# Running the first delta-rule chunks beside the input projection's last three column tiles

## The chip, the cores and the metric

One core of a Trainium2 chip runs the whole kernel. The metric is the device time of one execution in microseconds (us). A change counts as faster or slower here when two kernels, run alternately on the same chip, differ by more than what their runs scatter.

## The reference

The kernel computes one layer of a hybrid encoder for 16 + 2048 prompt rows and 64 sample rows, together 2128 rows. Cut to what matters here:

```python
h = rms_norm(x, attn_norm)
z = einsum('bld,dc->blc', h, w_in)          # ONE input projection
q_lat, kv_lat, k_rope_raw, qkv, gate, beta, a = split(z)
q = einsum(rms_norm(q_lat), w_uq)           # 8 attention heads
attn = chunk_causal_attention(q, k, v)      # k, v from kv_lat
u, k, v = causal_conv_silu(qkv) ...         # gated delta rule ("gdn")
for each chunk i:                           # a scan over the rows
    v_new = u_i - w_i @ S
    o     = (q_i * exp(g_i)) @ S + qk_i @ v_new
    S     = S * exp(g_last) + (k_i * exp(g_last - g_i)).T @ v_new
gdn = rms_norm(o) * silu(gate)
x = x + concat[rms_norm(attn), gdn] @ w_out
y = x + square(relu(rms_norm(x) @ w_up)) @ w_down
```

u, w and qk of a chunk come out of a triangular system of the chunk's own keys (its inverse is built by doubling), so they can be prepared ahead of the scan; only S runs from chunk to chunk.

## The kernel before

Matrix products are done in split numbers: each float operand is a high and a low part, and a product is three matmuls (high by high, high by low, low by high).

**The projection** (`phase_a`). The rows lie in five blocks of 336, 512, 512, 512 and 256. The 22 column tiles of the weight (128 columns each) are worked off in batches, in the order of the list `BATCHES`; for each batch a loop runs over the five blocks, and within a block over the batch's column tiles. `col_product` makes one column tile of one block: 8 x 3 = 24 matmuls into one PSUM bank `ps`. `col_finish` evicts it (L282, VectorE: `zt<-ps,rstd`), and for the output gate's tiles 17 to 20 a SiLU follows (three ScalarE activations L369 to L371, one VectorE product L372) and a store to `scr_gateT`. Tiles 0 to 2, the query latent, are followed by a norm: sums of squares, `mean_rstd` (a matmul into the small PSUM tile `ps_n`, L241), `rsqrt` (L141 to L146), three scalings (L325) and three stores to `scr_qlatT`. The six `zt` buffers go round, so an eviction waits until the store that last read its buffer is done. PSUM has eight banks: six go to `ps` (`APB`), two to `ps_n`. The last batches are `[0, 1, 2], [18], [19], [20]`: three times the five blocks, one gate tile after the other. `load_w` loads a column tile's weight in two halves (`wraw`), scales it (L258) and splits it (L134 on ScalarE, L135 on VectorE).

**The delta rule** (`phase_g`). 18 chunks are worked off by Python generators that are stepped round by round: `gdn_prep` (all that a chunk needs ahead of the scan: its keys' transposes L455, decay L461, norms L458 and L469, normed keys `kn` L485 and their transposes L489, products L498, the doubling with the tables `lev` L511 to L557, and at last `uf`), `gdn_scan` (the scan's first matmul is L598), and `q_gen`, the attention's queries (17 tiles x 18 matmuls L728 to L730 from the weight `wuq` and the stored query latent). Matmul results of `gdn_prep` go to five PSUM banks `gpp`, of the scan to two `gps`, and of `q_gen` to one `qp`. `q_gen`'s matmuls do not depend on the chunks and fill gaps. Attention, the output projection and the MLP follow.

**Who sets the order.** The Tile framework builds one instruction queue for each engine. A scheduler at build time sorts by dependencies and priorities (the order in which the program was written, if nothing else is said). On the chip each engine runs its queue in order: an instruction that waits holds up all behind it. Tiles come from pools. A pool that closes gives its SBUF or PSUM to pools opened later, whose first tiles then wait for the last reader of the old ones. In the kernel before, phase A's pools all close at its end, so `gpp` and most of the delta rule's SBUF take the place of the projection's.

Of the kernel before, what the change touches and what calls it, by code (L numbers as in the profile page):

```python
# [8 lines left out]
F32 = mybir.dt.float32  # L9
# [32 lines left out]
BATCHES = [[21, 3, 4]] + [[5 + i] for i in range(12)] + [[17], [0, 1, 2], [18], [19], [20]]  # L42
# [5 lines left out]
      "kneg": 3, "bh": 4, "bl": 4, "tt": 5, "uu": 5, "q16": 2, "rk": 3, "se": 1, "vw": 2, "S": 3, "o1": 1, "o": 1, "fr": 2}  # L48
GR, GK, GA, GF, GL0 = 6, 4, 5, 2, 4
QSB, QS = 2, 5  # L50
# [68 lines left out]
class Prog:  # L119
# [42 lines left out]
    def phase_a(self):  # L162
        nc, I = self.nc, self.I
        with ExitStack() as es:
# [7 lines left out]
            self.hp = self.pool(es, "h")  # L172
# [3 lines left out]
            self.aps = self.pool(es, "aps", space=PSUM)  # L176
# [35 lines left out]
    def load_x(self, b):  # L212
# [4 lines left out]
        hi = self.hp.tile([128, 8, n], F32R, name=f"hhi{b}")  # L217
        lo = self.hp.tile([128, 8, n], F32R, name=f"hlo{b}")
# [43 lines left out]
    def col_product(self, w, b):  # L262
# [5 lines left out]
        ps = self.aps.tile([128, NB], F32, name="ps", tag="ps", bufs=APB)  # L268
# [163 lines left out]
    def gt(self, tag, bufs=1, shape=(128, 4, 128), dt=F32):  # L432
        return self.gp.tile(list(shape), dt, name=tag, tag=tag, bufs=GB.get(tag, 1))

    def gpsum(self, kind="p"):
        return self.gps.tile([128, 4, 128], F32, name="gp" + kind, tag="gp" + kind, bufs=GPS[kind])
# [211 lines left out]
    def phase_g(self, g=True, q=True, eb=None):  # L648

        with ExitStack() as es:  # L650
            eq = es.enter_context(ExitStack())
            qp = self.pool(eq, "q", side="right")
            qps = self.pool(eq, "q_ps", space=PSUM, side="right")
            self.gp = self.pool(es, "g")
            self.gps = self.pool(es, "gps", space=PSUM)
            self.state = None
            self.lev = [[self.gp.tile([128, 4, 128], F16, name=f"lev{j}{i}") for i in range(7)] for j in range(NL)]
# [7 lines left out]
            while g and scanned < len(CHUNKS):  # L665

                if rounds >= max((started - GF) * GR, began[started % NL] + GL0) and len(preps) < GK and started < min(len(CHUNKS), scanned + GA):
                    preps.append(self.gdn_prep(CHUNKS[started], Ps[started]))
                    began[started % NL] = rounds
                    started += 1  # L670
                rounds += 1
                if rounds > QS:
                    if ek is not None:
                        if next(ek, "x") == "x" and self.first_prep is None:
                            self.first_prep = self.prep((0, 0, 0))
                            next(self.first_prep)
                    elif next(qg, "x") == "x" and eb is not None:
                        eq.close()
                        self.attn_early(eb)
                        ek = self.early_keys = self.keys(0, 0)  # L680
                if scan is None and "uf" in Ps[scanned]:
                    scan = self.gdn_scan(CHUNKS[scanned], Ps[scanned])
                if scan is not None and next(scan, "x") == "x":
                    scan, scanned = None, scanned + 1
                for p in list(preps):
                    if next(p, "x") == "x":
                        preps.remove(p)
# [346 lines left out]
    def attention(self):  # L1034
        with ExitStack() as es:
# [58 lines left out]
            while prep and prep[0][2] == 0:  # L1094
                prep_step()
# [835 lines left out]
```

## Time and profile before

| | |
|---|---|
| median of 3 runs | 3327.87 us (3316.88 to 3330.03) |
| the profiled execution | 3322.66 us |
| its span, first to last instruction | 3320.9 us |
| TensorE (PE) busy | 96% of the span |
| VectorE (DVE) busy | 80% |
| ScalarE (ACT) busy | 47% |
| GpSimd (POOL) busy | 12% |
| TensorE's granted clock, mean | 0.979 of 2.4 GHz |

TensorE is busy nearly all the time, but "busy" also holds time at half clock, in which the same work takes twice as long. In a row of the trace, the number in brackets at the end is how long the engine stood idle just before, and what released it.

### The profile page before, as it was taken

Reading aid. Unit: us, or ns where it says so; the run is one execution under the profiler, and the core shown is the slowest. Engines: PE = TensorE matmul, PEld = TensorE weight load, DVE = VectorE, ACT = ScalarE, POOL = GpSimd, SP = SyncE. Lnnn points to the kernel's source line nnn. Section 1 sums busy time; section 2 is a strip of 40 time slices with the busy share of each in tenths; the row PEclk is TensorE's granted clock in tenths of the full one; section 3 lists DMA queues with packets and bytes.
Section 4 is the critical chain, followed back from the end, with each engine's and each line's share of the span. In section 5 each row is a group of like instructions: output and inputs, shape, how many; then the busy total and the mean of one; then the engine's idle time right before and its main releaser. Section 6 shows DMA issues by size and latency. Waiting matters only on the chain.

```text
span 3320.9 us, 54512 instructions
## 1 busy us (share of the span) xinstructions
PE 3196.8 (96%) x20037; PEld 2943.1 (89%) x20037; DVE 2650.8 (80%) x5438; ACT 1558.4 (47%) x3495; POOL 400.5 (12%) x758
## 2 busy tenths in 40 slices
PE   9999998998979999999899999999999999999999
PEld 6888887888867778887799999999999999999999
DVE  8877654788758788888789888888888888988887
ACT  5555524555536868787564222334333333422232
POOL 0100013675510000000201000011000002100000
PEclk9999998999978999999999999999999999999999
DMA  4322213233221011010332222233222225122222
GB/s 132 91 74 70 74 63 100 87 104 100 59 57 35 20 34 34 25 37 26 106 99 75 77 77 75 76 110 109 88 76 73 65 73 160 58 73 77 77 74 70
DMA packets 318091, 248.09 MB, mean 75 GB/s; under 512 B 31776, under 2 KB 291616, under 8 KB 317760
## 3 DMA queue, kind: packets, MB, share of 16 engines
q1 hardware_dynamic: 300256, 219.21, 22.8%
q10 hardware_dynamic: 15536, 16.23, 1.6%
q0 software_dynamic: 2032, 9.18, 0.8%
q8 instruction: 157, 2.57, 0.3%
q14 instruction: 110, 0.90, 0.1%
HBM read 196.99 MB, written 47.52 MB: 74 GB/s over the span
## 4 chain that ended last, share of the span: by engine, by line
PE 83%; DVE 8%; ACT 2%; DMA 2%; issue 2%; POOL 1%; SPq 0%; POOLq 0%; DVEq 0%; ACTq 0%
PE psu L1601 23%; PE psd L1601 21%; PE ps L270 5%; PE ps L271 5%; PE ps L272 5%; PE pss L994 2%; PE pso L1011 2%; PE pss L995 2%; PE pss L996 2%; PE pso L1013 2%; PE pso L1012 2%; PE pspre L964 2%; DVE hl L1581 0%; PE psm L889 0%; DMA qh<-mrow 0%
## 5 line engine op out<-in xcount | busy, mean ns | idle before, releaser
L1601 PE MATMUL psu<-hh,uh 128*128 128x352 f32 x1728 | 563.0, 326 | 2.6 <-ACT uh L1497 2.1
L1601 PE MATMUL psu<-hl,uh 128*128 128x352 f32 x1728 | 557.3, 323 | 0.0
L1601 PE MATMUL psu<-hh,ul 128*128 128x352 f32 x1728 | 549.9, 323 | 0.0
L1601 PE MATMUL psd<-al,dh 128*128 128x352 f32 x1536 | 496.0, 323 | 3.5 <-DVE al L1790 3.2
L1601 PE MATMUL psd<-ah,dl 128*128 128x352 f32 x1536 | 494.6, 322 | 0.0
L1601 PE MATMUL psd<-ah,dh 128*128 128x352 f32 x1536 | 473.3, 324 | 11.1 <-DVE y L1709 7.4
L1709 DVE TENSOR_TENSOR y<-y,psd 128x352 f32<-128x352 f32 x768 | 386.6, 515 | 103.5 <-PE psd L1601 101.5
L1601 PEld LDWEIGHTS psu<-hh,uh 128*128 128x128 f32 x1728 | 325.7, 189 | 4.5 <-ACT uh L1497 2.5
L1601 PEld LDWEIGHTS psu<-hl,uh 128*128 128x128 f32 x1728 | 326.1, 189 | 1.2 <-issue 0.5
L1601 PEld LDWEIGHTS psu<-hh,ul 128*128 128x128 f32 x1728 | 323.9, 188 | 0.2 <-DVE ul L1475 0.2
L270 PE MATMUL ps<-hhi,whi 128*128 128x512 f32 (+5 forms) x880 | 313.6, 360 | 9.7 <-ACT hhi L134 7.1
L272 PE MATMUL ps<-hhi,wlo 128*128 128x512 f32 (+5 forms) x880 | 314.0, 358 | 0.0
L271 PE MATMUL ps<-hlo,whi 128*128 128x512 f32 (+5 forms) x880 | 312.5, 356 | 0.3 <-DVE hlo L135 0.2
L1601 PEld LDWEIGHTS psd<-ah,dh 128*128 128x128 f32 x1536 | 284.1, 188 | 16.9 <-DVE y L1709 11.5
L1601 PEld LDWEIGHTS psd<-al,dh 128*128 128x128 f32 x1536 | 289.1, 188 | 5.5 <-DVE al L1790 5.4
L1497 ACT CAST dh<-wr 128x512 fp32r<-128x512 f32 x192 | 119.3, 621 | 367.2 <-PE psd L1601 324.8
L1601 PEld LDWEIGHTS psd<-ah,dl 128*128 128x128 f32 x1536 | 288.8, 188 | 0.0
L1788 ACT CAST ah<-u 128x352 fp32r<-128x352 f32 x192 | 93.4, 487 | 398.6 <-DVE u L1786 280.0
L135 DVE TENSOR_TENSOR Pl<-P,Ph 128x512 fp32r<-128x512 f32 (+4 forms) x352 | 211.2, 611 | 52.2 <-ACT Ph L134 49.7
L998 ACT ACTIVATE P<-pss 128x512 f32<-128x512 f32 (+4 forms) x352 | 185.9, 539 | 87.6 <-PE pss L996 76.9
L965 DVE TENSOR_REDUCE mp<-pspre 128x1 f32<-128x296 f32 (+6 forms) x400 | 189.1, 500 | 31.1 <-PE pspre L964 29.2
L1714 POOL TENSOR_TENSOR y<-y,v 128x352 f32<-128x352 f32 x40 | 40.8, 1043 | 1330.8 <-DVE y L1709 1330.7
(458 smaller groups left out, 7266.5 us busy)
## 6 DMA issues: line engine op xcount, KB each, us to landing
wr<-in_w_up SPq DMA_DIRECT2D x192, 256.0 KB
wr<-in_w_down SPq DMA_DIRECT2D x192, 256.0 KB
qn<-scr_qN SPq DMA_DIRECT2D x32, 384.0 KB
wr<-in_w_out SPq DMA_DIRECT2D x48, 256.0 KB
wraw<-in_w_in SPq DMA_DIRECT2D x42, 256.0 KB
scr_convT<-s SPq DMA_DIRECT2D x36, 256.0 KB
mixr<-scr_mixT SPq DMA_DIRECT2D x12, 704.0 KB
out_y_T<-y SPq DMA_DIRECT2D x48, 176.0 KB
```

The costliest lines, as they stand in the source:

```text
L135: (lo_eng or nc.vector).tensor_tensor(lo, src, hi.bitcast(F32), op=ALU.subtract)
L270: nc.tensor.matmul(ps[:m, :n], whi[:, k, :m], hi[:, k], start=k == 0, stop=False)
L271: nc.tensor.matmul(ps[:m, :n], whi[:, k, :m], lo[:, k], start=False, stop=False)
L272: nc.tensor.matmul(ps[:m, :n], wlo[:, k, :m], hi[:, k], start=False, stop=k == 7)
L964: nc.tensor.matmul(ps[:, :z - a], qh[:r, i * 128:(i + 1) * 128], kh[:r, a:z], start=True, stop=True)
L965: nc.vector.tensor_reduce(m[:, i:i + 1] if one else mp[:, j:j + 1], ps[:, :z - a], axis=AX.X, op=ALU.max)
L994: nc.tensor.matmul(ps[:w, off:], kh[:r, s:s + w], qh[:r, off:], start=True, stop=False)
L998: nc.scalar.activation(p[:w, off:], ps[:w, off:], AF.Exp)
L1497: self.nc.scalar.copy(t[0], src)
L1601: self.nc.tensor.matmul(ps, w, h, start=i == 0, stop=i == len(steps) - 1)
L1709: adds.append(nc.vector.tensor_tensor(Y[j][:, d], Y[j][:, d], ps, op=ALU.add).ins)
L1788: done = nc.scalar.copy(A[f, j][0], u).ins
```

## The change

The three gate tiles 18, 19 and 20 become one batch, so that its loop goes block by block: tiles 18, 19, 20 of block 0, then of block 1, and so on. Their products no longer go into the six `ps` banks: that pool is closed ahead of the batch, and the products share the two banks of `ps_n`, in a pool on the other side of PSUM. So the delta rule's five `gpp` banks can be given out while the batch still runs. The split rows of each block (`hhi`, `hlo`) get a pool of their own, so that the SBUF of blocks 0, 1 and 2 comes free as the batch passes them; some buffers of the delta rule (the table `EG`) lie there, in the pool `g_early`. The scheduler gets a high priority for the first 2 steps of `q_gen` and the first 12 rounds of the delta rule, and another for the attention's first preparation.

```diff
-BATCHES = ... + [[17], [0, 1, 2], [18], [19], [20]]
+BATCHES = ... + [[17], [0, 1, 2], [18, 19, 20]]
+EG = {"kv": 2, "kq": 3, "lg": 1, "ss": 3, "sq": 1, "dm": 2, ...}
+HR, HO = 12, 360
+AO = 150
...
-            self.hp = self.pool(es, "h")
+            self.hp = [self.pool(es, f"h{b}") for b in range(len(BLOCKS))]
...
-            self.aps = self.pool(es, "aps", space=PSUM)
+            self.apn = self.pool(es, "apn", space=PSUM, side="right")
+            ea = es.enter_context(ExitStack())
+            self.aps = self.pool(ea, "aps", space=PSUM)
...
+                if not nxt:
+                    ea.close()
                 Wn = [self.load_w(ct) for ct in nxt[:3 - len(batch)]]
...
-                        ps = self.col_product(w, b)
+                        ps = self.col_product(w, b, n + 1 == len(BATCHES))
...
-        ps = self.aps.tile([128, NB], F32, name="ps_n", tag="psn", bufs=2)
+        ps = self.apn.tile([128, NB], F32, name="ps_n", tag="psn", bufs=2)
...
-        ps = self.aps.tile([128, NB], F32, name="ps", tag="ps", bufs=APB)
+        if last:
+            ps = self.apn.tile([128, NB], F32, name="ps", tag="psn", bufs=2)
+        else:
+            ps = self.aps.tile([128, NB], F32, name="ps", tag="ps", bufs=APB)
...
     def gt(self, tag, bufs=1, shape=(128, 4, 128), dt=F32):
-        return self.gp.tile(list(shape), dt, name=tag, tag=tag, bufs=GB.get(tag, 1))
+        k, n, e = self.gcount.get(tag, 0), GB.get(tag, 1), EG.get(tag, 0)
+        self.gcount[tag] = k + 1
+        early = k % n < e
+        return (self.ge if early else self.gp).tile(list(shape), dt, name=tag, tag=tag, bufs=e if early else n - e)
...
-            self.gps = self.pool(es, "gps", space=PSUM)
+            self.gps = {k: self.pool(es, "gp" + k, space=PSUM) for k in "ps"}
...
-            for _ in range(QP):
-                next(qg, None)
+            with self.tc.high_priority(HO):
+                for _ in range(QP):
+                    next(qg, None)
...
+                with ExitStack() as early:
+                    if rounds < HR:
+                        early.enter_context(self.tc.high_priority(HO))
...
-            while prep and prep[0][2] == 0:
-                prep_step()
+            with self.tc.high_priority(AO):
+                while prep and prep[0][2] == 0:
+                    prep_step()
```

Every engine runs the same instructions in both kernels (TensorE 21013 of them, VectorE 5438); only their order, their buffers and their waits differ. Line numbers after the change are 9 to 21 higher. Three places of the built queues show it.

TensorE, where the last batches begin. `ps_4447` is tile 18 of block 0 in the kernel before, `ps_4480` and `ps_4513` are the same tile of blocks 1 and 2; shown are the first matmul of each product and, of the first product, where the norm's matmul stands:

```order
L272 MATMUL ps_4370<-hhi4_772,wlo_3895 128x256
L270 MATMUL ps_4447<-hhi0_126,whi_4423 128x336 [waits DVE_49,Activation_49]
...
L241 MATMUL ps_n_4397<-sq_4308,ones_64 128x512 [waits Pool_49]
...
L270 MATMUL ps_4480<-hhi1_249,whi_4423 128x512
...
L270 MATMUL ps_4513<-hhi2_403,whi_4423 128x512
```

After the change `ps_4475`, `ps_4508` and `ps_4541` are tiles 18, 19 and 20 of block 0, and `ps_4592` and `ps_4625` tiles 18 and 19 of block 1:

```order
L250 MATMUL ps_n_4412<-sq_4323,ones_64 128x512 [waits DVE_49,Pool_49]
L282 MATMUL ps_4475<-hhi0_141,whi_4438 128x336 [waits DVE_49,Activation_49]
...
L282 MATMUL ps_4508<-hhi0_141,whi_4450 128x336 [waits DVE_49,Activation_49]
...
L282 MATMUL ps_4541<-hhi0_141,whi_4462 128x336 [waits DVE_49,Activation_49]
...
L250 MATMUL ps_n_4574<-sq_4430,ones_64 128x256 [waits DVE_49]
L282 MATMUL ps_4592<-hhi1_264,whi_4438 128x512 [waits DVE_49]
...
L282 MATMUL ps_4625<-hhi1_264,whi_4450 128x512 [waits DVE_49]
```

The third product now waits for VectorE (its bank was the first product's), as does every one behind it; before, the second and third products waited for nothing of VectorE's.

VectorE after the change, at the same place. `zt_4500` and `zt_4533` evict tiles 18 and 19 of block 0; the rows ahead belong to the weight of tile 20 and to the query latent's norm:

```order
L151 TENSOR_TENSOR nr_4417<-nr_4417,nt_4415 128x512 [waits DVE_49]
L140 TENSOR_TENSOR wlo_4463<-wraw_4464,whi_4462 128x512 [waits Activation_49]
L140 TENSOR_TENSOR wlo_4463<-wraw_4469,whi_4462 128x512 [waits Activation_49]
L337 SCALAR_TENSOR_TENSOR zt_4249<-zt_4249,g_qa_93,nr_4417 128x512 [waits DVE_49]
L337 SCALAR_TENSOR_TENSOR zt_4276<-zt_4276,g_qa_93,nr_4417 128x512
L337 SCALAR_TENSOR_TENSOR zt_4303<-zt_4303,g_qa_93,nr_4417 128x512
L319 TENSOR_TENSOR sq_4430<-sq_4430,sq_4435 128x256 [waits Activation_49]
L294 TENSOR_TENSOR zt_4500<-ps_4475,rstd_128 128x336 [waits DMAHW7_49,DVE_49,PE_49]
L294 TENSOR_TENSOR zt_4533<-ps_4508,rstd_128 128x336 [waits DMAHW0_49,DVE_49,PE_49]
```

The first eviction of the batch stands behind the same scalings and waits for the same store as in the kernel before (there it is `zt_4472<-ps_4447`, also the 628th row of VectorE's queue); it did not move.

TensorE, where the projection ends and the delta rule begins. Before, `ps_4939` is the last product, `gpp_5021` the first chunk's transposes, `gpp_5095` the transposes of its normed keys, `qp_5319` the first query product:

```order
L270 MATMUL ps_4939<-hhi4_772,whi_4630 128x256 [waits DVE_49]
...
L455 MATMUL gpp_5021<-ident_59,kv_5014 16x128 [waits DMAHW2_49,DVE_49]
...
L461 MATMUL gpp_5076<-m_le_72,lg_5054 128x128 [waits Pool_49]
...
L489 MATMUL gpp_5095<-ident_59,kn_5063 128x16 [waits DVE_49,Activation_49]
...
L728 MATMUL qp_5319<-wuq_h_5004,ql_h_5262 128x384 [waits Activation_49]
```

After the change the same chunk's steps are `gpp_5047` (L470), `gpp_5102` (L476, of the second chunk) and `gpp_5121` (L504); `ps_4823` and `ps_4856` are tiles 19 and 20 of block 3, `ps_4889`, `ps_4922` and `ps_4955` tiles 18 to 20 of block 4, `gpp_5305` the transposes of the third chunk's normed keys, `qp_5345` the first query product, `gps_5745` the first scan:

```order
L470 MATMUL gpp_5047<-ident_59,kv_5040 16x128 [waits DMAHW5_49]
...
L282 MATMUL ps_4823<-hhi3_604,whi_4450 128x512 [waits DVE_49]
...
L476 MATMUL gpp_5102<-m_le_72,lg_5080 128x128 [waits Pool_49]
...
L282 MATMUL ps_4856<-hhi3_604,whi_4462 128x512 [waits DVE_49]
...
L504 MATMUL gpp_5121<-ident_59,kn_5089 128x16 [waits DVE_49,Activation_49]
...
L282 MATMUL ps_4955<-hhi4_787,whi_4462 128x256
...
L504 MATMUL gpp_5305<-ident_59,kn_5278 128x128 [waits DVE_49,Activation_49]
...
L749 MATMUL qp_5345<-wuq_h_5030,ql_h_5288 128x384 [waits Activation_49]
...
L613 MATMUL gps_5745<-vn_5087,uf_5657 16x128
```

The first two chunks' first steps have moved ahead of five of the fifteen products, which now stand between them. The query products moved back: 63 of their matmuls stand ahead of the first scan before, 9 after. The weight `wuq`, which they need, is loaded by SyncE's queue behind three more chunks' keys than before.

## Rows read from the trace of the kernel before

**Rows 1.** Busy us of each engine by stretch of the span, with granted clock:

```profile
core 0: us, PE busy (x) PEld busy (x) DVE busy (x) ACT busy (x) POOL busy (x), PEclk, DMA share, GB/s
450.00:500.00 50.00, 50.00 (x279) 43.98 (x278) 33.07 (x55) 18.88 (x35) 4.30 (x3) 1.00 0.28 99
500.00:530.00 30.00, 30.00 (x153) 25.95 (x152) 7.82 (x13) 11.36 (x20) 0.28 (x1) 1.00 0.25 72
...
540.00:550.00 10.00, 2.05 (x16) 1.59 (x14) 7.28 (x18) 5.13 (x26) 6.41 (x15) 0.82 0.79 247
550.00:560.00 10.00, 9.19 (x45) 8.12 (x45) 6.94 (x13) 4.04 (x8) 6.62 (x6) 0.50 0.43 112
560.00:570.00 10.00, 7.80 (x50) 6.48 (x49) 6.59 (x12) 6.65 (x23) 9.26 (x15) 0.84 0.28 74
570.00:580.00 10.00, 10.00 (x64) 8.52 (x63) 4.06 (x10) 4.43 (x19) 5.64 (x14) 0.65 0.16 31
...
590.00:600.00 10.00, 9.78 (x95) 8.53 (x96) 6.10 (x16) 4.09 (x15) 3.64 (x9) 0.83 0.20 61
```

**Rows 2.** Timeline of TensorE: start us, us, engine, line, operation:

```profile
538.81 0.60 PE L455 MATMUL gpp<-ident,kv 128*16 128x128 f32 x4
...
550.46 0.57 PE L489 MATMUL gpp<-ident,kn 16*128 16x16 f32 x4 [8.11 <-DVE kn L485]
...
565.41 0.40 PE L529 MATMUL gpp<-id,lev 128*128 128x128 f16 x4 [0.95 <-DVE lev L521]
...
569.60 1.08 PE L489 MATMUL gpp<-ident,kn 128*128 128x128 f32 x4 [1.15 <-DVE kn L485]
...
585.82 0.40 PE L529 MATMUL gpp<-id,lev 128*128 128x128 f16 x4 [1.35 <-DVE lev L521]
...
590.19 0.44 PE L728 MATMUL qp<-wuq_h,ql_h 128*128 128x384 f32 x1 [1.07 <-ACT qsq L732]
...
597.27 0.39 PE L598 MATMUL gps<-vn,uf 16*16 16x128 f32 x2
```

**Rows 3.** Timeline of VectorE behind the projection's end:

```profile
541.61 2.10 DVE L511 COPY lev<-id 128x512 f16<-128x512 f16 x10
...
544.45 2.53 DVE L469 TENSOR_SCALAR rk<-ss 16x4 f32<-16x4 f32 x2
549.64 0.68 DVE L485 TENSOR_TENSOR kn<-gpp,rk 16x512 f32<-16x512 f32 x1 [2.66 <-POOL rk L146]
```

**Rows 4.** Groups of TensorE's instructions between 468.76 and 538.81 us:

```profile
L270 PE MATMUL ps<-hhi,whi 128*128 128x512 f32 x72 | 28.2, 392 | 0.0
...
L270 PE MATMUL ps<-hhi,whi 128*128 128x336 f32 x24 | 8.0, 333 | 0.0
...
L270 PE MATMUL ps<-hhi,whi 128*128 128x256 f32 x24 | 6.8, 282 | 0.0
```

**Rows 5.** Timeline of TensorE, first matmul of tile 18:

```profile
468.76 0.32 PE L270 MATMUL ps<-hhi,whi 128*128 128x336 f32 x1
```

**Rows 6.** Timeline of VectorE at that batch's start:

```profile
472.20 1.28 DVE L135 TENSOR_TENSOR wlo<-wraw,whi 128x512 fp32r<-128x512 f32 x2
...
482.28 2.07 DVE L325 SCALAR_TENSOR_TENSOR zt<-zt,g_qa,nr 128x512 f32<-128x512 f32 x3
485.19 0.51 DVE L282 TENSOR_TENSOR zt<-ps,rstd 128x336 f32<-128x336 f32 x1 [0.84 <-DMA scr_qlatT<-zt]
```

**Rows 7.** Timeline of SyncE's queue, DMA issues:

```profile
472.91 0.93 SPq L256 DMA_DIRECT2D wraw<-in_w_in  x2
483.06 1.65 SPq L327 DMA_DIRECT2D scr_qlatT<-zt  x3
...
541.87 0.82 SPq L700 DMA_DIRECT2D qs<-in_w_uq  x2
```

**Rows 8.** Timeline of ScalarE, weight of tile 20:

```profile
477.73 1.27 ACT L134 CAST whi<-wraw 128x512 fp32r<-128x512 f32 x2 [1.62 <-DVE wraw L258]
```

**Rows 9.** Timeline of ScalarE, query weight's high part:

```profile
552.60 1.57 ACT L134 CAST wuq_h<-qs 128x768 fp32r<-128x768 f32 x2
```

More of the change, by code (lines that the diff above doesn't have):

```diff
@@ L41 @@
 RUNS = [(0, 1), (1, NS), (NS, NS + 1), (NS + 1, 18)]
-BATCHES = [[21, 3, 4]] + [[5 + i] for i in range(12)] + [[17], [0, 1, 2], [18], [19], [20]]
+BATCHES = [[21, 3, 4]] + [[5 + i] for i in range(12)] + [[17], [0, 1, 2], [18, 19, 20]]
 WRB, APB, ZTB, XTB = 2, 6, 6, 4
@@ L216, in load_x @@
         n = b1 - b0
-        hi = self.hp.tile([128, 8, n], F32R, name=f"hhi{b}")
-        lo = self.hp.tile([128, 8, n], F32R, name=f"hlo{b}")
+        hi = self.hp[b].tile([128, 8, n], F32R, name=f"hhi{b}")
+        lo = self.hp[b].tile([128, 8, n], F32R, name=f"hlo{b}")
         self.h.append((hi, lo))
@@ L260, in load_w, with col_product @@
         return hi, lo, m
-    def col_product(self, w, b):
+    def col_product(self, w, b, last=False):
         nc = self.nc
@@ L432, in gt @@
     def gt(self, tag, bufs=1, shape=(128, 4, 128), dt=F32):
[L433 removed]
+        k, n, e = self.gcount.get(tag, 0), GB.get(tag, 1), EG.get(tag, 0)
+        self.gcount[tag] = k + 1
+        early = k % n < e
+        return (self.ge if early else self.gp).tile(list(shape), dt, name=tag, tag=tag, bufs=e if early else n - e)
     def gpsum(self, kind="p"):
[L436 removed]
+        return self.gps[kind].tile([128, 4, 128], F32, name="gp" + kind, tag="gp" + kind, bufs=GPS[kind])
     def gdn_prep(self, n, P):
@@ L653, in phase_g @@
             qps = self.pool(eq, "q_ps", space=PSUM, side="right")
+            self.ge, self.gcount = self.pool(es, "g_early"), {}
             self.gp = self.pool(es, "g")
-            self.gps = self.pool(es, "gps", space=PSUM)
+            self.gps = {k: self.pool(es, "gp" + k, space=PSUM) for k in "ps"}
             self.state = None
-            self.lev = [[self.gp.tile([128, 4, 128], F16, name=f"lev{j}{i}") for i in range(7)] for j in range(NL)]
+            self.lev = [[self.ge.tile([128, 4, 128], F16, name=f"lev{j}{i}") for i in range(7)] for j in range(NL)]
             qg = self.q_gen(qp, qps) if q else iter(())
             ek = None
-            for _ in range(QP):
-                next(qg, None)
+            with self.tc.high_priority(HO):
+                for _ in range(QP):
+                    next(qg, None)
             Ps = [{"first": i < NL} for i in range(len(CHUNKS))]
@@ L665, in phase_g @@
             while g and scanned < len(CHUNKS):
[L667 to L687, printed above, removed]
+                with ExitStack() as early:
+                    if rounds < HR:
+                        early.enter_context(self.tc.high_priority(HO))
+                    if rounds >= max((started - GF) * GR, began[started % NL] + GL0) and len(preps) < GK and started < min(len(CHUNKS), scanned + GA):
+                        preps.append(self.gdn_prep(CHUNKS[started], Ps[started]))
+                        began[started % NL] = rounds
+                        started += 1
+                    rounds += 1
+                    if rounds > QS:
+                        if ek is not None:
+                            if next(ek, "x") == "x" and self.first_prep is None:
+                                self.first_prep = self.prep((0, 0, 0))
+                                next(self.first_prep)
+                        elif next(qg, "x") == "x" and eb is not None:
+                            eq.close()
+                            self.attn_early(eb)
+                            ek = self.early_keys = self.keys(0, 0)
+                    if scan is None and "uf" in Ps[scanned]:
+                        scan = self.gdn_scan(CHUNKS[scanned], Ps[scanned])
+                    if scan is not None and next(scan, "x") == "x":
+                        scan, scanned = None, scanned + 1
+                    for p in list(preps):
+                        if next(p, "x") == "x":
+                            preps.remove(p)
```

2 lines of the change are left out of this document (added).

## The prediction

> **What bounds the kernel now.** TensorE is busy for 96% of the span, so a change of order pays only where TensorE stands idle or runs at its lower clock. I read the busy time by stretches first [rows 1]. Up to 530 us TensorE is busy without a gap at granted clock 1.00. From 540 to 550 it is busy for 2.05 of 10 us, and then the clock is 0.50 (1.2 instead of 2.4 GHz) for a whole stretch, and lower than 1.00 in three of the next four. The timeline of TensorE [rows 2] names the place: the projection's last matmul ends where the first chunk's transposes start, at 538.81, and after a few of them the engine stands for 8.11 us until `kn`, the normed keys, arrives from VectorE; `kn` itself ends a chain of small steps over four engines (squares, `rk` at 544.45, GpSimd's `rsqrt`, `kn` at 549.64, with 14 copies of the table `lev` in front of it, the last ten of them from 541.61) [rows 3]. Four more waits of the same kind follow, 0.95, 1.15, 1.35 and 1.07 us, before the first scan starts at 597.27 [rows 2].
>
> **What the change can win.** Between 538.81 and 597.27 the waste is:
> - idle: 8.11 + 0.95 + 1.15 + 1.35 + 1.07 = 12.6 us [rows 2];
> - half clock: of each stretch's busy time, the share of the clock that was not granted: 9.19 x 0.50 + 7.80 x 0.16 + 10.00 x 0.35 + 9.78 x 0.17 = 4.6 + 1.2 + 3.5 + 1.7 = 11.0 us [rows 1].
>
> Together 23.6 us. Since TensorE runs the same matmuls in both kernels, this is all that the start of the delta rule can give back. That 54 of the query's matmuls move behind the first scan is neither gain nor loss in this account: it makes the first scan earlier, and they are done later.
>
> After the change the chain from the first transposes to `kn` lies beside products: between them the queue holds tile 19 of block 3 whole and 14 of the 24 matmuls of tile 20. The price of a product follows from its columns. The fifteen products from 468.76 to 538.81 [rows 4, 5, 2] have 9 x 512 + 3 x 336 + 3 x 256 = 6384 columns in 70.05 us, 0.011 us a column: 5.6 us for 512 columns, 3.7 for 336, 2.8 for 256. So 5.6 x 38/24 = 8.9 us of products and some 2 us of other steps stand where 8.11 us of idle time stood, and I count that wait as gone, with the half clock behind it. `lev`'s copies have moved ahead of the chain.
>
> It is not all gone. From the last product (`ps_4955`) to the first scan the queue now has 9 query matmuls where before they filled the gaps, and the doubling of the first chunks is a chain through VectorE and ScalarE. Waits like the 4.5 us that stood there in spite of the filler [rows 2] will be there again: at least 0, at most twice as much and a stretch at half clock of 3.5 us [rows 1], so 0 to 12; I take 5, near what stood there. That leaves a gain of 18.6 us.
>
> **What the change adds.** The products of the last batch now have two PSUM banks. Follow the start of the batch. Tile 18 of block 0 starts at 468.76 [rows 5] and takes 3.7 us. Tile 19 of block 0 needs the low part of its weight, which VectorE makes from 472.20 to 473.48 [rows 6], and so ends at about 473.4 + 3.7 = 477.1. Tile 20 needs the bank of tile 18, thus its eviction. In the kernel before that eviction comes at 485.19 only [rows 6], 12.7 us after the product's end, and this costs nothing because five more banks are free: TensorE is busy all the time [rows 1]. What it waits for is a store: its `zt` buffer is read by the query latent's store, issued at 483.06 [rows 7] behind the scalings at 482.28 [rows 6], which stand behind a weight of the batch that was issued at 472.91 [rows 7]. In the changed queue of VectorE the same instructions stand in front of it and it waits for the same store, so I see no reason for it to be earlier. Tile 20 starts at 485.19 + 0.51 = 485.7: a new wait of 8.6 us. Behind it the next product, tile 18 of block 1, needs tile 20's eviction, which stands behind two sums of the gate: about 1 us more. From then on a product (5.6 us) is longer than an eviction, and two banks do. Sum: 9.6 us. Of this 1.5 us would be there with any number of banks, as the weight of tile 20 is cast from 477.73 [rows 8].
>
> Bounds: below, only that 1.5 us, if the order on the chip lets the eviction be earlier; above, 12, if each of the next products in block 0 and 1 waits for 1 us too. After the wait I expect a stretch at half clock, as after the 8.11 us: 4.6 us [rows 1], between 0 and the 9.3 that all of 550 to 580 cost. The sum of what is added is 9.6 + 4.6 = 14.2 us.
>
> A rule speaks against the change here. The Trainium skill (Perfetto Trace Analysis, Matmuls and Matmul Optimizations) says that independent groups of matmuls should rotate through the PSUM banks, so that the eviction of one overlaps the next, and that all eight should be used. By that rule alone the sum would be a loss of the 14.2 us. The trace agrees for block 0, where the eviction comes 12.7 us after its product; in later blocks, where it follows within a product's time, no row shows that more than two are needed.
>
> The edits that cost nothing: the pool of each block and `g_early` issue no instructions, and the g phase's buffers lie in blocks that the batch has passed; the priority `AO` leaves the attention's first matmuls where they were; the gate's SiLU and stores are the same in number and lie beside products of 2.8 to 5.6 us (uncovered, an eviction costs what the row of 0.51 us shows, once a product [rows 6]).
>
> **Sum.** 14.2 added - 18.6 won = -4.4 us. Against the profiled execution of 3322.66 us that is 3318.3; the runs' median is 5.2 us higher, and against it 3323.5 us, which is my forecast.
>
> **The rivals.**
> 1. *The wait for the bank is short, or the clock stays up.* For it: the 8.6 us rest on one eviction in a queue of before. Against: the same 627 instructions stand in front. With 1.5 us of wait and no half clock the gain is 18.6 - 1.5 = 17.1; with the idle time but full clock it is 9.0. Faster: 3308 to 3319.
> 2. *Slower: the query's weight comes late and stops VectorE.* In the queue of VectorE the low part of `wuq` stands in the middle of the doubling, and its loads are now issued behind three more chunks' keys. Before, the loads were issued at 541.87 [rows 7] and first used at 552.60 [rows 9], so they may take up to 10.7 us. If the keys' buffer that the last of these loads waits for comes free only when the third chunk is under way, VectorE stands up to 10.7 us with the doubling behind it, and TensorE, which has no filler there, with it, and a half clock stretch of 4.6 follows. That is 15.3 - 4.4 = 11 us slower, 3339; from a standstill of about 3 us on the gain is gone. Two such loads in sequence would pass 0.5%.
> 3. *It does not do what it says*: the first chunks' steps wait for SBUF or keys that come no earlier, and the products merely stand somewhere else: the 8.11 us stay, in several pieces. Then there is the 14.2 us of loss against some of the gain: within 10 us of before, 3330 to 3337.
>
> **How the numbers follow.** Forecast (3317 to 3330) 0.52, rival 1 0.28, rival 2 0.10, rival 3 0.10. About 0.5%, 16.6 us, is what a measurement of this kernel can tell from no change: under 3311.3 is faster, over 3344.5 slower. Rival 1 gives three quarters of its chance to faster, the forecast a little: 0.23. Slower takes half of rival 2 and some of rival 3: 0.08. The rest is the same: 0.69. The range goes from rival 1's better end to where rival 3 ends: 3307 to 3336; outside are the worst of rival 2 and a gain of the whole 23.6 us with scatter.
>
> **What would show it.** In the profile after: a wait of 8 to 9 us of TensorE near 477 us, ended by an eviction of VectorE, with about 1 us behind it and a stretch at half clock from 486 on; the first transposes of the delta rule near 533 instead of 538.81, and no wait above 3 us for `kn`; the first scan between 580 and 590 (4.4 us and the 54 query matmuls earlier). The prediction is wrong if there is no wait at 477 (then rival 1), if TensorE waits over 4 us for the doubling or VectorE for `wuq` (rival 2), or if the first scan is not earlier than 594 (rival 3).

## The result: 0.8% slower, and the profile after

The changed kernel takes 3351.59 us (median of 5 runs, 3343.8 to 3357.22). The kernel before takes 3321.56 us (median of 5 runs). The ratio is 1.0082, with a 95% interval of 1.0061 to 1.0103. The forecast was 3323.5 us with a range to 3336, and 0.08 for slower: wrong, and with the wrong sign.

The page of the changed kernel, its span and TensorE's busy time:

```profile
span 3355.5 us, 54531 instructions
PE 3223.1 (96%) x20037; PEld 2965.0 (88%) x20037; DVE 2646.8 (79%) x5438; ACT 1553.0 (46%) x3495; POOL 398.8 (12%) x758
```

TensorE executes as many instructions as before, in 26 us more of busy time. Since a busy TensorE at half clock also counts as busy, that is the first hint of where to look.

The start first. Busy time by stretches of the changed kernel (columns as in [rows 1]):

```profile
470.00:480.00 10.00, 8.13 (x50) 7.48 (x48) 9.61 (x19) 4.72 (x9) 0.00 (x0) 1.00 0.30 105
480.00:490.00 10.00, 6.25 (x25) 6.25 (x26) 4.64 (x10) 2.75 (x6) 0.00 (x0) 0.66 0.31 115
...
560.00:570.00 10.00, 8.44 (x90) 6.76 (x89) 8.08 (x21) 5.21 (x22) 7.45 (x11) 1.00 0.63 183
570.00:580.00 10.00, 8.54 (x82) 6.12 (x81) 7.66 (x18) 5.62 (x13) 5.61 (x6) 0.53 0.39 126
580.00:590.00 10.00, 10.00 (x75) 8.08 (x72) 3.27 (x10) 3.54 (x10) 2.10 (x3) 0.50 0.09 22
590.00:600.00 10.00, 10.00 (x59) 6.85 (x59) 5.22 (x12) 2.07 (x7) 2.23 (x9) 0.60 0.16 53
```

and TensorE's timeline, where the third product waits for its bank, where the delta rule begins, where the query's weight is waited for, and the first scan:

```profile
483.75 0.62 PE L282 MATMUL ps<-hhi,whi 128*128 128x336 f32 x1 [5.63 <-DVE zt L294]
...
528.77 0.60 PE L470 MATMUL gpp<-ident,kv 128*16 128x128 f32 x4
...
577.48 0.69 PE L750 MATMUL qp<-wuq_l,ql_h 128*128 128x384 f32 x1 [1.33 <-DVE wuq_l L140]
...
583.08 0.60 PE L613 MATMUL gps<-vn,uf 16*16 16x128 f32 x2
```

Up to the first scan the change does what was forecast. There is a new wait of 5.63 us for the bank, the 8.11 us for `kn` [rows 2] are gone, the delta rule begins 10 us earlier (528.77, 538.81 before) and the first scan 14.2 us earlier (583.08, 597.27 before). But from 570 to 600 TensorE's granted clock is 0.50 to 0.60, so it runs mostly at the lower of its two levels (0.50).

What follows is lost later. The table gives the starts of five matmuls in the profiled execution of each kernel, in us: the first, eleventh and fifteenth scan, the attention's first score matmul (`pspre`), the MLP's first matmul (`psu`). The last column is the mean time between scans 11 and 15. An execution of one kernel can differ from its median: the one profiled is 12.4 us below it for three banks, and 11.0, 8.9 and 5.6 us above it for no priority, seven buffers and the changed kernel; the others lie within 3 us.

| kernel | scan 1 | scan 11 | scan 15 | attention | MLP | per chunk |
|---|---|---|---|---|---|---|
| before | 597.27 | 829.54 | 898.12 | 949.6 | 1683.0 | 17.1 |
| changed | 583.08 | 836.59 | 921.69 | 977.3 | 1715.5 | 21.3 |
| priority on 6 rounds | 584.14 | 820.09 | 888.57 | 942.6 | 1678.3 | 17.1 |
| batch alone | 596.34 | 834.13 | 908.62 | 961.5 | 1703.6 | 18.6 |
| one by one | 588.83 | 823.27 | 891.87 | 946.8 | 1687.4 | 17.1 |
| no priority | 601.43 | 840.93 | 928.17 | 984.0 | 1723.7 | 21.8 |
| five banks | 594.81 | 830.73 | 904.86 | 959.3 | 1692.5 | 18.5 |
| three banks | 579.15 | 822.01 | 905.85 | 961.3 | 1693.7 | 21.0 |
| seven buffers | 583.07 | 825.05 | 901.67 | 953.8 | 1707.7 | 19.2 |
| 6 rounds, no `AO` | 585.33 | 820.99 | 891.47 | 944.3 | 1676.7 | 17.6 |
| filler | 587.86 | 841.70 | 912.62 | 965.5 | 1713.0 | 17.7 |

The changed kernel leads by 14.2 us at the first scan and is 27.7 us behind at the attention. Where the lead goes can be read from scans 1, 9 and 11. Before:

```profile
597.27:792.26 194.99, 179.08 (x1742) 160.92 (x1739) 157.11 (x328) 106.81 (x378) 125.48 (x256) 0.96 0.36 101
792.26:829.54 37.28, 34.70 (x389) 32.04 (x388) 30.84 (x73) 20.95 (x75) 20.71 (x35) 0.95 0.33 84
```

and after:

```profile
583.08:790.50 207.42, 188.56 (x1743) 168.83 (x1742) 152.78 (x313) 104.83 (x374) 127.87 (x265) 0.94 0.32 92
790.50:836.59 46.09, 38.70 (x404) 36.58 (x404) 36.20 (x86) 23.78 (x91) 23.78 (x44) 0.91 0.39 105
```

At scan 9 the changed kernel is still 1.8 us ahead (790.50, 792.26 before): up to there it has lost the 9.7 us of the query matmuls that the start left behind, and 2.7 more. The two chunks from scan 9 to 11 cost another 8.8 us, the four from scan 11 to 15 cost 16.5, what follows up to the attention 4.1. So most of the loss comes after the query's last matmul, at 774.3. The counts in the brackets show that a little of it is postponed work: some 30 matmuls of the attention's first steps (tiles `psm`), which ran ahead of scan 9 before, now run between scans 9 and 15.

Take the four chunks between scans 11 and 15, where the query's matmuls are all done. Busy time from scan to scan, in the kernel before:

```profile
829.54:846.51 16.97, 15.55 (x186) 14.38 (x185) 13.06 (x29) 9.09 (x34) 9.93 (x17) 1.00 0.31 80
846.51:864.32 17.81, 15.80 (x186) 14.31 (x185) 13.40 (x31) 9.10 (x34) 10.02 (x17) 1.00 0.30 75
864.32:881.24 16.92, 15.56 (x187) 14.39 (x186) 13.01 (x29) 9.09 (x34) 9.91 (x17) 1.00 0.19 49
881.24:898.12 16.88, 15.55 (x186) 14.38 (x185) 12.52 (x30) 8.99 (x34) 8.97 (x16) 1.00 0.19 48
```

and in the changed kernel:

```profile
836.59:857.33 20.74, 18.62 (x199) 17.56 (x199) 16.01 (x36) 10.69 (x39) 10.13 (x18) 0.91 0.31 79
857.33:877.85 20.52, 18.37 (x189) 16.98 (x189) 12.42 (x30) 8.68 (x34) 9.81 (x17) 0.83 0.28 73
877.85:901.27 23.42, 19.41 (x186) 18.23 (x185) 13.21 (x28) 8.80 (x34) 9.89 (x17) 0.79 0.14 35
901.27:921.69 20.42, 17.15 (x186) 15.96 (x185) 13.59 (x28) 8.77 (x34) 8.79 (x16) 0.92 0.16 40
```

Look at the second and third column (the time of a chunk and how long TensorE is busy in it), at the count behind them and at the clock. In the last two rows of each, TensorE executes the same 186 matmul instructions. Before, a chunk takes 16.9 us: 15.55 busy at full clock and 1.35 idle. After, it takes 20.4 to 23.4: 3.3 to 4.0 idle, and a clock of 0.79 to 0.92.

Nothing in the diff touches the steps of these chunks: their preparation begins 36 rounds and more behind the priority of the first 12 rounds, and instructions and number of buffers are the same. (The higher counts in the changed kernel's first two rows, 199 and 189, come from transposes of the attention's first steps.) What differs is the order in which the scheduler repeats a chunk's steps. TensorE before, part of one chunk (L627 is the scan's second output product, L455 the transposes of a later chunk's keys, L489 those of its normed keys):

```profile
870.64 0.64 PE L455 MATMUL gpp<-ident,kv 128*128 128x128 f32 x4
...
872.00 1.06 PE L627 MATMUL gps<-vw,qk 128*128 128x128 f32 x8
...
877.35 0.63 PE L489 MATMUL gpp<-ident,kn 128*128 128x128 f32 x4 [0.43 <-ACT wt L580]
```

and after (L642 is that output product, L470 and L504 the two transposes):

```profile
864.24 1.11 PE L642 MATMUL gps<-vw,qk 128*128 128x128 f32 x8
...
866.32 0.63 PE L470 MATMUL gpp<-ident,kv 128*128 128x128 f32 x4
...
871.41 2.05 PE L593 MATMUL gpp<-uf,kneg 128*128 128x128 f32 x8
873.25 0.63 PE L556 MATMUL gpp<-tt,bh 128*128 128x64 f16 x8
875.21 1.09 PE L504 MATMUL gpp<-ident,kn 128*128 128x128 f32 x4 [1.32 <-DVE fr L649]
```

The scan's output product has moved ahead of the keys' transposes, and the next chunk's two groups of key products (L498, now L513) from ahead of the scan to behind its first matmuls. So the squares of the scan's output now come ahead of the keys' squares on ScalarE. Before:

```profile
871.31 0.28 ACT L458 ACTIVATE sq<-gpp 128x128 f32<-128x128 f32 x1
...
874.07 0.33 ACT L632 ACTIVATE o<-o 128x128 f32<-128x128 f32 x1
```

After:

```profile
866.11 0.31 ACT L647 ACTIVATE o<-o 128x128 f32<-128x128 f32 x1 [1.05 <-DVE o L644]
...
867.48 0.29 ACT L647 ACTIVATE o<-o 128x128 f32<-128x128 f32 x1
...
867.77 0.26 ACT L473 ACTIVATE sq<-gpp 128x128 f32<-128x128 f32 x1
```

From the keys' transposes to those of the normed keys it is 6.7 us before (870.64 to 877.35) and 8.9 us after (866.32 to 875.21), with the output product's 0.9 us of cover gone from in between. L593 (L578 before), which makes the product of `uf` and `kneg`, takes 2.05 us in this chunk where it took 1.14 before: TensorE runs at the lower level of its clock there.

The place of the key products tells the two orders apart in every trace. In the kernel before they stand ahead of the next scan in each chunk from the fourth scan to the fourteenth. In the changed kernel they stand behind the scan's first matmuls from the third scan on; up to scan 9, while the query's matmuls still stand between a chunk's steps, the net loss is the 2.7 us named above.

### The profile page after: what moved, and what is told of

Same layout as the page of the kernel before. It is cut to its first block, busy times and chain, and to the rows that moved or that the text cites. A ratio compares the mean times of both kernels' runs of the same rounds, so it can differ in the third digit from the quotient of the medians.

```text
span 3355.5 us, 54531 instructions
## 1 busy us (share of the span) xinstructions
PE 3223.1 (96%) x20037; PEld 2965.0 (88%) x20037; DVE 2646.8 (79%) x5438; ACT 1553.0 (46%) x3495; POOL 398.8 (12%) x758
## 4 chain that ended last, share of the span: by engine, by line
PE 84%; DVE 8%; ACT 2%; DMA 2%; issue 2%; POOL 1%; SPq 0%; POOLq 0%; ACTq 0%; DVEq 0%
PE psu L1623 23%; PE psd L1623 21%; PE ps L282 5%; PE ps L283 5%; PE ps L284 5%; PE pss L1015 2%; PE pso L1032 2%; PE pss L1016 2%; PE pso L1034 2%; PE pss L1017 2%; PE pso L1033 2%; PE pspre L985 2%; DMA mixr<-scr_mixT 0%; PE gps L613 0%; PE gpp L513 0%
## 5 line engine op out<-in xcount | busy, mean ns | idle before, releaser
L1623 PE MATMUL psd<-ah,dh 128*128 128x352 f32 x1536 | 473.8, 324 | 11.1 <-DVE y L1731 7.4
L1623 PEld LDWEIGHTS psd<-ah,dh 128*128 128x128 f32 x1536 | 284.6, 188 | 16.9 <-DVE y L1731 11.5
L282 PEld LDWEIGHTS ps<-hhi,whi 128*128 128x128 f32 (+1 forms) x880 | 165.1, 188 | 42.5 <-issue 7.6
```

Source lines behind the costliest of these rows:

```text
L282: nc.tensor.matmul(ps[:m, :n], whi[:, k, :m], hi[:, k], start=k == 0, stop=False)
L1623: self.nc.tensor.matmul(ps, w, h, start=i == 0, stop=i == len(steps) - 1)
```

## The experiments

There were two theories. **A**: the time is lost in the chunk loop, because the scheduler, which at build time settles on a repeating order of a chunk's steps, settled on a worse one; which order it finds depends on small things at the start. **B**: something that the change does costs the time, the two banks, the split pools and early buffers, or the query matmuls that were moved. The built queues show the repeating order of any kernel, so kernels could be chosen by it. In the traces the key products stand where they stood before in experiments 1, 3 and 8; they stand behind the scan's first matmuls from the ninth scan on in experiments 2, 4 and 5, from the eleventh in 6 (and in its third chunk), from the seventh in 7 and from the third in 9.

**1. Priority on 6 rounds.** All of the change, but the scheduler's priority ends earlier:

```diff
-HR, HO = 12, 360
+HR, HO = 6, 360
```

> The changed kernel with the high priority on the first 6 rounds of the delta rule instead of 12; pools, banks, buffers and the batch of three tiles are those of the change, and the start of the queue is the same up to block 4. In the built queue the repeating order of TensorE's steps in the later chunks is again that of the kernel before. Theory A (the time is lost in the chunk loop, because the scheduler settled there on another repeating order): scans 11 to 15 follow each other at 17.1 us (+-0.5) as before, not at 21.3, and the time is 3305 to 3320 us, 0.995 to 1.000 of before. Rival B (the buffers in the early pool, the split PSUM pools or the two banks slow the loop): intervals of 20 to 21.5 us and 3345 to 3357 us. Both expect the wait of 5.6 us for the bank near 478 us.

Measured: 3318.8 us, ratio 0.9995 (0.9986 to 1.0004). Chunks from scan to scan, in that kernel:

```profile
837.20:854.80 17.60, 15.84 (x187) 14.35 (x186) 13.30 (x29) 9.10 (x34) 9.99 (x17) 1.00 0.30 76
854.80:871.70 16.90, 15.54 (x187) 14.37 (x185) 12.99 (x29) 9.09 (x34) 9.91 (x17) 1.00 0.19 49
871.70:888.60 16.90, 15.58 (x187) 14.41 (x186) 12.63 (x30) 9.09 (x34) 8.97 (x16) 1.00 0.19 48
```

The loop of the kernel before is back, at full clock, with the two banks, the pools and the batch of three still in place. The wait for the bank is there too (5.59 us). So B falls for the banks and the buffers as the cause of the loop's loss. The kernel differs from the changed one in more than the loop, though: 27 query matmuls stand ahead of its first scan instead of 9, and in the 17 us behind it the clock is 1.00, not 0.56. Of the 34.7 us by which it leads the changed kernel at the attention, 16.6 are gained between scans 11 and 15 and 17.6 between scans 1 and 11.

**2. The batch alone.** The kernel before with one edit:

```diff
-... + [[17], [0, 1, 2], [18], [19], [20]]
+... + [[17], [0, 1, 2], [18, 19, 20]]
```

> The kernel before with one edit: tiles 18, 19 and 20 in one batch, block by block; six banks, one pool for the rows, no early pool, no priorities. The delta rule starts behind the projection, as before. The built queue settles in the chunk loop on an order like the changed kernel's (the two groups of key products stand behind the scan's first matmuls, not ahead of its last transposes). Theory A: start as before (a wait of about 8 us for the normed keys, first scan near 597 us), but scans 11 to 15 at 19 to 21.5 us and 3335 to 3352 us. Rival B: none of the pools is there, so 17.1 us a chunk and 3316 to 3328 us.

Measured: 3343.09 us, ratio 1.0058 (1.0045 to 1.0072). Two of its chunks:

```profile
869.96:889.19 19.23, 16.56 (x187) 15.47 (x185) 13.30 (x30) 9.07 (x36) 10.49 (x18) 0.92 0.18 43
889.19:908.62 19.43, 17.28 (x186) 16.22 (x185) 11.84 (x28) 8.68 (x34) 8.76 (x16) 0.85 0.18 42
```

Its delta rule starts where it did before (first scan 596.34), none of the change's pools or priorities is there, and still the loop is slow (18.6 us a chunk over all four, a little under the expected 19). A holds; the loss is smaller than the changed kernel's.

**3. One by one.** The changed kernel with tiles 18, 19 and 20 as three batches (the edit is number 2's, backwards).

> The changed kernel with the batches of the kernel before, 18, 19 and 20 one after the other; only the last of them goes into the two banks and beside the delta rule. Pools, early buffers and priorities are those of the change. Its chunk loop has the order of the kernel before. Theory A: 17.1 us a chunk and 3312 to 3326 us, since little of the start is covered. Rival B: 20 to 21.5 us a chunk, 3345 us and more.

Measured: 3328.96 us, ratio 1.0017 (1.0008 to 1.0027). 17.1 us a chunk, as A expects; but 0.2% slower than before, above the expected range, though it leads by 2.8 us at the attention. It loses 7 us between the attention's start and the MLP's (see what stays open).

**4. No priority.** The changed kernel with `HR, HO = 0, 0`.

> The changed kernel without the high priority of the first 12 rounds and of the first two query steps. The query's matmuls stand ahead of the first scan nearly as before, and the loop's order is the changed kernel's. Theory A: 20 to 21.5 us a chunk, first scan between 585 and 597 us, 3338 to 3355 us. Rival C (the loss comes from the query's matmuls that the priority moved behind the first scan): 17 us a chunk once the query is done and 3312 to 3326 us.

Measured: 3355.13 us, ratio 1.0108 (1.0091 to 1.0125). Three of its chunks:

```profile
840.93:860.00 19.07, 15.84 (x202) 14.88 (x201) 12.74 (x30) 9.37 (x36) 10.17 (x18) 1.00 0.28 71
860.00:882.60 22.60, 18.60 (x186) 17.48 (x185) 13.44 (x29) 9.19 (x36) 10.53 (x18) 0.82 0.23 59
882.60:906.00 23.40, 19.39 (x186) 18.28 (x185) 13.22 (x28) 8.77 (x34) 9.88 (x17) 0.79 0.14 35
```

63 query matmuls stand ahead of its first scan, as in the kernel before, and its loop is as slow as the changed kernel's (21.8 us a chunk, a little above what I expected, as is the time). So the moved query matmuls are not the cause of the loop's loss. The first scan, at 601.43, came later than I expected: without the priority TensorE waits 4.28 us for `kn` at 553.38 again, and the wait for the bank (5.49 us) is paid for nothing.

**5. Five banks.** The kernel before, with one number changed that has nothing to do with the delta rule:

```diff
-WRB, APB, ZTB, XTB = 2, 6, 6, 4
+WRB, APB, ZTB, XTB = 2, 5, 6, 4
```

> The kernel before with one number changed: five PSUM banks for the projection's products instead of six. No batch, no pools, no priorities; TensorE's queue is the same up to the last projection products. But the built queue settles, in the later chunks, on the repeating order that the batch alone gave (key products behind the scan's first matmuls). Theory A (the order of the loop costs the time, and anything that nudges the scheduler can choose it): first scan within 3 us of 597.3, scans 11 to 15 at 18.5 to 20.5 us instead of 17.1, and 3332 to 3348 us. Rival B (something of the change itself is needed for the slow loop): 17.1 us a chunk and 3316 to 3328 us.

Measured: 3335.23 us, ratio 1.004 (1.0028 to 1.0053). The four chunks from scan 11 to 15:

```profile
830.73:847.78 17.05, 14.76 (x166) 13.81 (x165) 12.07 (x27) 7.94 (x33) 9.34 (x17) 0.97 0.32 79
847.78:869.11 21.33, 19.18 (x206) 18.10 (x205) 12.71 (x31) 9.81 (x37) 10.88 (x19) 0.82 0.25 63
869.11:887.37 18.26, 16.02 (x186) 15.10 (x185) 12.30 (x28) 8.28 (x33) 9.15 (x17) 0.96 0.18 46
887.37:904.86 17.49, 15.25 (x186) 14.32 (x185) 12.51 (x29) 8.67 (x35) 8.74 (x17) 1.00 0.19 46
```

Nothing of the change is in this kernel. Its first scan is 2.5 us earlier than before, and at the attention it is 9.7 us behind. This is the plainest case for A. The first chunk leaves 20 matmuls to the second. The last row shows the order's cost at full clock: 17.5 us for 186 matmuls, 0.6 more than the order before, with 2.2 us idle instead of 1.35. Over the four chunks this kernel takes 5.6 us more than the kernel before: 2.8 of that is idle time and 2.7 is busy time, for the same number of matmuls at a lower clock.

**6. Three banks.** The changed kernel with `bufs=3` for `psn` and `APB` 5, so that tile 20 of a block has a bank of its own at first.

> The changed kernel with three banks instead of two for the last batch (and five instead of six for the batches ahead). The order of the chunk loop is the changed kernel's. If the wait near 478 us is for the bank, it falls from 5.6 us to under 3 (the weight of tile 20 and the fourth product remain), and the first scan comes 2 to 6 us earlier than 583; scans 11 to 15 stay at 20 to 21.5 us; in all 3341 to 3350 us. If the bank is what makes the change slow, the time falls to 3330 us or less.

Measured: 3344.43 us, ratio 1.0069 (1.0054 to 1.0085). The wait for the bank is gone; what is left is one for the weight of tile 20:

```profile
483.35 0.65 PE L284 MATMUL ps<-hhi,wlo 128*128 128x336 f32 x1 [2.35 <-DVE wlo L140]
```

The first scan comes 3.9 us earlier than in the changed kernel, and the chunks from scan 11 to 15 stay at 21.0 us. So in this kernel the third bank is worth some 4 us at the start, and the change is not slow because it has two. (The order is the changed kernel's only from the eleventh scan on, so this is not a comparison of banks alone.)

**7. Seven buffers.** The changed kernel with `ZTB, XTB = 7, 3`.

> The changed kernel with seven buffers for the evicted tiles instead of six (and three instead of four for the norm's scratch, to make room). The first eviction of the batch then waits for an earlier store, and the scheduler puts it nine places further ahead in VectorE's queue. If that eviction was held by its buffer's store, it comes near 478 us instead of 483.1 and TensorE's wait for the bank falls from 5.6 to under 2.5 us. The loop's order is that of the batch alone, so 18.5 to 20.5 us a chunk and 3335 to 3350 us.

Measured: 3339.76 us, ratio 1.0053 (1.0035 to 1.0071). VectorE's first eviction of the batch:

```profile
479.28 0.50 DVE L294 TENSOR_TENSOR zt<-ps,rstd 128x336 f32<-128x336 f32 x1
```

The same eviction in the changed kernel, behind its buffer's store:

```profile
483.10 0.51 DVE L294 TENSOR_TENSOR zt<-ps,rstd 128x336 f32<-128x336 f32 x1 [0.50 <-DMA scr_qlatT<-zt]
```

So it comes 3.8 us earlier, and TensorE has no wait for it: the store of its buffer, and its place behind the norm, did hold it. Yet the first scan starts at 583.07, where it started in the changed kernel: TensorE waits 2.50 us for a sum of squares at 471.56 instead of 0.24, the clock is 0.50 from 570 on, and 18 query matmuls stand ahead of the scan instead of 9. The loop takes 19.2 us a chunk, as its order let expect.

**8. 6 rounds, no `AO`.** Number 1 with `AO = 0`.

> The changed kernel with the high priority on 6 rounds and without the priority of the attention's first preparation. If that priority does nothing, as the prediction said, the time is that of the run with 6 rounds, 3314 to 3322 us, and the stretch from the attention's first matmul to the MLP's first lasts 733 to 738 us as there (735.7). If it costs what the run with 6 rounds lost behind the delta rule (its lead of 7 us at the attention's first matmul had fallen to 4.7 at the MLP's), it is 2 to 4 us faster.

Measured: 3317.85 us, ratio 0.9988 (0.9979 to 0.9997). From the attention's first matmul to the MLP's it takes 732.4 us, 735.7 in number 1. The medians of the two kernels lie within 1 us; the ratios to the kernel before, 0.9988 and 0.9995, differ by 2.3 us, but their intervals overlap. So the priority costs 2 us or nothing; the two are not told apart. This is the only version whose interval ends below 1, and its gain is 0.1%. It has the order of the kernel before, and still one of its chunks was slow, after a wait of 2.00 us at 849.49:

```profile
838.13:857.49 19.36, 16.82 (x186) 15.77 (x185) 13.12 (x29) 9.09 (x34) 10.03 (x17) 0.91 0.27 69
```

**9. Filler.** The changed kernel with 24 matmuls of constants more in each chunk; what they write is overwritten:

```diff
         tkn = self.gpsum()
+        for _ in range(6):
+            for h in range(4):
+                nc.tensor.matmul(tkn[:, h, :], self.id16, self.id16, start=True, stop=True)
         for h in range(4):
             nc.tensor.transpose(tkn[:, h, :C], kn[:C, h, :], ...)
```

> The changed kernel with 24 matmuls more in each chunk, of constants, into the bank of the normed keys' transposes and ahead of them; the transposes overwrite what they write, so the outputs do not change. They are about 1.3 us of TensorE's time a chunk at full clock (24 x 0.055), 24 us over 18 chunks if nothing else changes. The scheduler places them ahead of the inverse's matmuls and of the normed keys' transposes, in the order that the batch alone gave. If it is the gaps of TensorE in the loop that lower its clock, the filler keeps it at 0.95 or more between scans 11 and 15, and with 1.3 us of more work a chunk they take 18 to 19.5 us instead of 21.3; in all 3335 to 3355 us. If the clock falls for another reason, the filler comes on top: 20.5 to 22.5 us a chunk, clock 0.80 to 0.92, 3355 to 3380 us.

Measured: 3352.64 us, ratio 1.0087 (1.0071 to 1.0104). The four chunks from scan 11 to 15:

```profile
841.70:860.84 19.14, 17.99 (x227) 16.99 (x226) 14.10 (x33) 10.13 (x38) 11.22 (x20) 1.00 0.36 95
860.84:878.10 17.26, 16.43 (x211) 15.60 (x209) 12.31 (x28) 8.73 (x35) 9.81 (x18) 1.00 0.29 77
878.10:895.36 17.26, 16.43 (x211) 15.60 (x209) 12.46 (x29) 8.81 (x35) 9.77 (x18) 1.00 0.20 48
895.36:912.62 17.26, 16.44 (x211) 15.60 (x209) 12.49 (x29) 8.77 (x35) 8.75 (x17) 1.00 0.20 48
```

With 24 matmuls more, three chunks take 17.26 us each and the mean of the four is 17.7, less than I expected, and the clock is 1.00. The chunks of 186 matmuls in the order of numbers 2 and 5, without the filler, took 17.49 to 19.43 us at clocks of 1.00 to 0.85. So the clock stayed up where the gaps were closed (0.83 us idle a chunk, 2.2 to 2.7 there). Two things closed them, and the run doesn't separate them: the filler, and the normed keys' transposes, which in the trace stand behind three of the four groups of another chunk's doubling products instead of ahead of them. In number 5 TensorE waits for those keys in each of the last two chunks:

```profile
903.46 0.63 PE L489 MATMUL gpp<-ident,kn 128*128 128x128 f32 x4 [1.42 <-DVE kn L485]
```

With the filler that wait is gone. The order is not the changed kernel's either, so what its own loop would gain at full clock isn't shown. As a whole the kernel gains nothing: its first scan is 4.8 us later than the changed kernel's, it takes as long to the eleventh (from 769 to 842 us at clocks of 0.85 to 0.92, in spite of the filler), and the attention takes 747.5 us.

## Why the prediction was wrong

**The step that failed** is that the sum ends at the first scan. The prediction says of the waste up to there that "this is all that the start of the delta rule can give back", which may stand, and then sets the chunks behind it at nothing, without a reason: I took it that they, which the change does not touch, would run as before. They did not: the scheduler repeated their steps in another order. From the first scan to the attention the changed kernel takes 394.2 us, 41.8 more than the 352.4 before. Of that, 9.7 is query matmuls that the start left behind (54 of some 0.18 us), 2.7 is what else is lost up to scan 9, 8.8 the two chunks from there to scan 11, 16.5 the chunks from scan 11 to 15 and 4.1 those behind them. The 2.7 is a net figure: right behind the first scan TensorE ran for 16.92 us at a clock of 0.56, some 7.4 us of loss, part of which was made up later. Between scans 11 and 15, 5.4 of the 16.5 us is idle time and 11.1 is busy time, most of it the lower clock. Experiments 1, 2, 4 and 5 show that the order goes with the loop's loss, and not the banks, the buffers, the batch or the priority. The order stands in the built queue, of which the prediction uses only the start.

**The rivals.** The first was right that the wait would be shorter than 8.6 us, but the gain that it drew from this was lost behind the first scan. The slower one (the query's weight stops VectorE) did not decide: TensorE waited 1.33 us for that weight. The third was wrong too, as the start did move. None of the three named the loop.

**Point by point at the start.**
- *The 8.11 us wait goes, hidden by products*: right. The longest wait of the start behind the products was 1.53 us for `kn`.
- *A new wait near 477 us for the bank, 8.6 us and 1 more*: right in place and cause, too large. It was 5.63, and 0.17 for the next product. VectorE did the same steps, but the eviction came at 483.10 instead of 485.19, since the norm's three scalings, which stand in front of it, began at 480.20 instead of 482.28; and the product ahead of the wait ended at 478.1, 1 us later than in the sum, as the batch itself began 1.4 us later (470.15, 468.76 before). Experiments 6 and 7 removed the wait in two ways.
- *4.6 us of half clock behind it*: about 2.1 (6.25 us at 0.66).
- *First transposes near 533, first scan between 580 and 590*: 528.77, 583.08.
- *5 us of the waste stays, for lack of filler*: too small. From 561, where the last product ends, to the first scan TensorE was idle for 3.0 us and lost 5.3 to the clock (19.05 us busy at 0.72); another 7.4 followed behind the first scan, where I had let the clock recover.
- *`AO` costs nothing*: experiment 8 finds 2 us or nothing.
- *The net gain of 4.4 us*: at the first scan the lead is 14.2 us, and 4.5 without the 9.7 of postponed query matmuls. That the sum comes out there is luck: what the change adds was 7.9 us (5.63, 0.17 and 2.1) instead of 14.2, the waste that stays was 9 (3.9 of idle time from 528.77 on, 5.3 of clock) instead of 5, and the later start of the batch was not in the sum. With the old loop order (experiment 1) the kernel leads by 7.0 us at the attention and by 4.7 at the MLP; its ratio is 0.9995, which its interval does not tell from 1.

The rule of the Trainium skill (Perfetto Trace Analysis, Matmuls) that products should rotate through the banks pointed to a real wait: 5.63 us. Without it the first scan came 3.9 us earlier in experiment 6 and no earlier in experiment 7. The rule did not point to the loss of 30 us.

**What stays open.** The stretch from the attention's first matmul to the MLP's takes 732 to 742 us in most profiled executions (733.4 before, 738.2 changed, 740.6 in experiment 3), 747.5 in experiment 9 and 753.9 in experiment 7. No experiment was made on it, and whether order, clock or chance of the execution makes these differences isn't known; it is 4.9 of the changed kernel's 32.5 us at the MLP's start. That the squares on ScalarE are what lengthens the chain of normed keys in the slower order was read from one chunk's timeline and not tried by itself. No experiment changes the order alone: each edit picks another build, in which the start, or the place of other work, differs as well. That the order causes the loss rests on its going with it in all eleven kernels.

## What to carry to other kernels

Where a scheduler at build time orders a software pipeline, an edit at its start can change the order of the whole loop, and the loop is where the time is: compare the repeating rows of the built queue, not only the place of the edit, and try one or two neighbours of each constant (6 rounds instead of 12 gave back 30 us here) before judging the idea. A change of one number with no bearing on the loop (five banks for six) cost 0.4%, so a single measured build says little about the idea that it carries.

## What was not expected of the hardware

- The clock: in the changed kernel's last two chunks before scan 15, 3.3 and 4.0 us of idle time in 20.4 and 23.4 us went with a granted clock of 0.92 and 0.79, and 1.35 us in 16.9 before with 1.00. No single wait in those chunks was longer than 1.45 us; at the start, 5.63 and 8.11 us in one piece went with 0.66 (480 to 490 us) and 0.50 (550 to 560 in the kernel before). Idle time alone does not settle it: a chunk of experiment 4 was idle for 3.2 of 19.07 us at 1.00.
- Three kernels with the changed kernel's order (changed, no priority, three banks) took the same 23.4 us at 0.79 for one chunk. But the order does not fix every chunk: the order of experiments 2 and 5 took 17.49 to 19.43 us for 186 matmuls, and the old order took 19.36 us at 0.91 once, in experiment 8.
- With 24 matmuls more in each chunk, and the normed keys' transposes later, the chunks of experiment 9 took 17.26 us at 1.00, less than any chunk of 186 matmuls in experiments 2 and 5.
